# Eight gate projections of the first attention branch computed as four pairs of quarter products, `mid` emitted one step later, and all copies of transposed probabilities on ScalarE

## The chip, the cores and the metric

The kernel runs on one core of one Trainium2 chip. The metric is the device time of the program in microseconds (us); lower is better. A core has five engines that each work through their own queue of instructions in order: TensorE (PE in the profile; its weight loads are listed apart as PEld), VectorE (DVE), ScalarE (ACT), GpSimd (POOL) and SyncE (SP), which here issues most of the DMA transfers. Engines wait for each other through semaphores.

## The reference

One layer of a streaming encoder, for 1024 tokens of a new stream (prompt) and 64 tokens of a running one (sample, with 512 cached tokens), all in float32. The model width is 1024, and each branch has 8 heads of 64.

```python
h = rms_norm(x, norm_w) @ w_in            # 6144 columns:
# sb_q sb_k sb_v sb_z (512 each) | cb_q cb_k cb_v cb_z (512 each) | g_sb g_cb (1024 each)

def stick_breaking(q, k, v):              # first branch, "sb": all earlier keys
    z = q @ k.T * 0.125
    # weight[t,s] = sigmoid(z[t,s]) * product over s<j<t of (1 - sigmoid(z[t,j]))

def band_attention(q, k, v, rel_bias):    # second branch, "cb": nine chunks of 64 keys
    s = q @ k.T * 0.125 + bias            # q and k normed per head
    p = softmax(s)

b_sb = (o_sb * silu(z_sb)) @ w_proj_sb
b_cb = (o_cb * silu(z_cb)) @ w_proj_cb
y = x + (sigmoid(g_sb) * b_sb + sigmoid(g_cb) * b_cb) @ w_out
```

It also returns new keys and values of both branches. The cached keys and the relative bias are scaled up, so that scores are large.

## The kernel before

Every float32 operand of a projection is split into a high part (rounded to the fast matmul format) and a low part (the rest), and a product is made as high x high + high x low + low x high. So a product over 128 rows takes three matmuls. "Prep" of a weight block is a ScalarE copy (high) and a subtraction on GpSimd (low).

The program runs through these stages:

1. **Normed tokens and natural projections** (matmuls at L464): RMSNorm, transposes, and the columns whose result is wanted with tokens on partitions (values of both branches, queries and keys of the second).
2. **Quarter products** (L544 to L658; matmuls at L634): a list `pairs` of column blocks of 256. The block is cut in two halves of columns, the tokens in two halves, the contraction in two halves, and the eight quarter products that this would need are replaced by seven products of sums and differences (a Strassen scheme). Each product has two chunks of tokens (256 and 288 columns), four steps of contraction and three matmuls a step. Before the change `pairs` holds eight entries: keys and queries of the first branch (kinds `"k"`, `"q"`) and the SiLU gates of both branches (`"silu"`). `emit` (L565) evicts a result by its kind, and its code for a kind `"sig"`, a sigmoid without the multiplication, is there already. `prep` and `presum` (L391 to L437) make the operands, `load_raw` (L379) loads the weights, and after the last pair the first gate unit (`load_unit(0)`).
3. **Attention** (L663 to L1205). The tokens are nine tiles: eight of 128 and the sample's 64, called t = 8. The list `seq` (L991) has 144 steps, in the order branch, pair of heads, tile (the sample first), head: 72 of the first branch, then 72 of the second. A step's row length is 128 to 1024 columns in the first branch and 128 to 640 in the second.
4. **Merging and output projection** (L1207 on).

A step of attention is spread over several turns of the loop at L1169:

- `qk(i)` (L1002): scores on TensorE (L1024, L1025). In the first branch ScalarE takes two sigmoids of them (L1027 into `kp`, L1028 into `be`). In the second VectorE adds the bias and finds the row's extreme (L1030), and ScalarE takes the exponential with its sum (L1034).
- `mid(i)` (L1037), on VectorE alone: in the first branch a scan over the row (L1044) and a multiplication (L1045), in the second a reciprocal (L1047) and a scaling (L1048).
- `tr(i)` (L1055), three turns after `qk(i)` (`LAG = 3`): transposes of the probabilities on TensorE into PSUM (L1076) and copies into `wT`. A counter `flip` gives each copy to ScalarE (L1085) or VectorE (L1087): of the first branch's every fourth goes to VectorE, of the second's every other one.
- `av` (L1096): weights times values for two tiles and both heads (L1115), then one multiplication with the SiLU gate on VectorE (L1118).
- `fill(n)` (L978): `n` matmuls from a generator, `run_fill` (L766), which hold TensorE busy between these. The generator first computes gate `units`, one block of 128 columns each, with 72 matmuls (three chunks of tokens with 384, 384 and 320 columns, eight steps of contraction, three matmuls; L773). `ev_act` (L745) evicts a chunk with one ScalarE activation (L748) and stores it. Behind the units it starts the first branch's projection (L873, evicted on VectorE at L877). Before the change there are 16 units, eight of each branch.

One turn `i` emits, in this order: `qk(i)`, loads, half of the turn's filler, `av` if two tiles are complete, `tr(i-3)`, `mid(i)`, the other half of the filler. Each engine executes what it is given in the order of emission. Six calls of `fill(24)` ahead of the loop (two units) cover the first loads.

How much filler a turn gets is written out by hand: `n_sb` matmuls over the first branch and `n_cb` (and 24 more) over the second, shared out by row length (`wt`, `tot`, `amount`, L1161 to L1190). `FP` = 180 is the part of the projection that is reached inside the loop; the rest follows after it (L1278). One more rule: `fill` holds the last unit back, and owes its matmuls, until the flag `late["sb"]` is set at L1191, in the sixth step of the second branch, because the last unit starts loads of the first branch's results (L775).

```python
                        if ci == k == n == 0 and j + 1 == len(units):
                            load_og("sb", 0, late["y"])
...
        while n > 0:
            if prog[0] == len(units) - 2 and "sb" not in late:
                owed[0] = n
                return
```

Scores in PSUM have three buffers (`psZ`), transposes two (`psT`), `be` four, `kp` three and `wT` four.

Of the kernel before, what the change touches and what calls it, by code (L numbers as in the profile page):

```python
# [10 lines left out]
AF = mybir.ActivationFunctionType  # L11
# [6 lines left out]
KT = 8  # L18
# [14 lines left out]
def hybrid_step_kernel(ctx: ExitStack, tc: tile.TileContext, x_prompt, x_sample, c_sbk, c_sbv, c_cbk, c_cbv,  # L33
# [3 lines left out]
    V, A, G, TE, SP = nc.vector, nc.scalar, nc.gpsimd, nc.tensor, nc.sync  # L37
# [15 lines left out]
    def rows(t):  # L53
        return 128 if t < 8 else NS
# [26 lines left out]
    d_g = {b: [dram.tile([128, T], F32, name=f"d_g{b}{u}") for u in range(KT)] for b in ("sb", "cb")}  # L81
# [63 lines left out]
    pairs = []  # L145
    for p in (0, 2):
        pairs += [("k", 512 + 128 * p, p), ("q", 128 * p, p)]
    for p in (0, 2):
        pairs += [("silu", 1536 + 128 * p, d_z["sb"][p:p + 2]), ("silu", 3584 + 128 * p, d_z["cb"][p:p + 2])]
    units = [("ev_act", 4096 + 128 * j, (AF.Sigmoid, d_g["sb"][j])) for j in range(KT)]  # L150
    units += [("ev_act", 5120 + 128 * j, (AF.Copy, d_g["cb"][j])) for j in range(KT)]

    def put_t(dst, src):
        A.activation(dst[0], src, AF.Copy)
# [43 lines left out]
    with ExitStack() as ph:  # L198
# [251 lines left out]
        for i in range(nb):  # L450
            for ti, t in enumerate(TO):
                r = rows(t)
# [6 lines left out]
                for m, (k, n) in enumerate(steps):  # L459
                    if i == 0 and ti == 0 and m == 4:  # L460
                        prep_b(0)
                    w = W.sp[i, k // 4][n // (ns - 1)][:, k % 4]
# [81 lines left out]
    with ExitStack() as ph:  # L544
# [70 lines left out]
        for i in range(len(pairs)):  # L615
            bank, s1, u2, u3 = {}, {}, {}, {}
            for s in range(7):
# [8 lines left out]
                w = blk.pop(n)  # L626
                for c, (a, b) in enumerate(XC):
                    m = b - a
# [22 lines left out]
                if s == 4:  # L651
                    for c, (a, b) in enumerate(XC):
                        m = b - a
# [324 lines left out]
    def fill(n):  # L978
        n += owed[0]
        owed[0] = 0  # L980
        while n > 0:
# [9 lines left out]
    seq = [(b, p, t, hd) for b in ("sb", "cb") for p in range(NPAIR) for t in [8] + list(range(8))  # L991
           for hd in range(2)]

    def band(b, t):
        if t == 8:
            return 0, 576
        if b == "sb":
            return 0, (t + 1) * 128
        k0 = max(0, t - 4)
        return k0, (t + 1 - k0) * 128  # L1000

    def qk(i):  # L1002
        b, p, t, hd = seq[i]
        key = (b, p)
        r = rows(t)
        k0, n = band(b, t)
        hs = [(0, n)] if n <= 512 else [(0, n // 2), (n // 2, n)]
        be = am.tile([128, NP], F32, name="be", bufs=4)
        if t == 8:
            s, ks, q0 = SQ[key, 3], KS[key, 1], 0  # L1010
        else:
            s, ks, q0 = SQ[key, t // 3], KS[key, 0], (t % 3) * 128
        if b == "sb":
            kp = ax.tile([128, NP + 2], F32, name="kp", bufs=3)
            G.memset(kp[:r, n:n + 1], 0.0)
        else:
            kp = am.tile([128, 4], F32, name="sm", bufs=6)
            bt = BI[2 * p + hd]
            off = 0 if t == 8 else 640 - n
        for j, (x, y) in enumerate(hs):  # L1020
            z = psZ.tile([128, 512], F32, name="z")
            o = k0 * 128
            m = y - x
            TE.matmul(z[:r, :m], s[:, 2 * hd, q0:q0 + r], ks[:, hd, o + x:o + y], start=True, stop=False)  # L1024
            TE.matmul(z[:r, :m], s[:, 2 * hd + 1, q0:q0 + r], ks[:, hd, o + x:o + y], start=False, stop=True)  # L1025
            if b == "sb":
                A.activation(kp[:r, x:y], z[:r, :m], AF.Sigmoid, scale=-0.125)  # L1027
                A.activation(be[:r, x:y], z[:r, :m], AF.Sigmoid, scale=0.125)  # L1028
            else:
                V.tensor_tensor_reduce(be[:r, x:y], z[:r, :m], bt[:r, off + x:off + y], 1.0,  # L1030
                                       BIG if j == 0 else kp[:r, j - 1:j], OP.add, OP.min, kp[:r, j:j + 1])
        if b == "cb":
            j = len(hs) - 1
            A.activation(be[:r, :n], be[:r, :n], AF.Exp, bias=kp[:r, j:j + 1], scale=-1.0, accum_out=kp[:r, 2:3])  # L1034
        st[i] = (be, kp)

    def mid(i):  # L1037
        b, p, t, hd = seq[i]
        r = rows(t)
        k0, n = band(b, t)  # L1040
        be, kp = st[i]
        if b == "sb":
            im = imp[0:64, 960 - n:960] if t == 8 else imp[:, NP - n:NP]
            V.tensor_tensor_scan(kp[:r, n - 1::-1], kp[:r, n - 1::-1], im[:, ::-1], 0.0, op0=OP.mult, op1=OP.add)  # L1044
            V.tensor_tensor(out=be[:r, :n], in0=be[:r, :n], in1=kp[:r, 1:n + 1], op=OP.mult)  # L1045
        else:
            V.reciprocal(kp[:r, 3:4], kp[:r, 2:3])  # L1047
            V.tensor_scalar(be[:r, :n], be[:r, :n], kp[:r, 3:4], None, op0=OP.mult)  # L1048

    def wbase(b, j):  # L1050
        return max(0, 2 * j - 4) if b == "cb" and j < 4 else 0

    flip = [0]

    def tr(i):  # L1055
        b, p, t, hd = seq[i]
        r = rows(t)
        k0, n = band(b, t)
        be, _ = st.pop(i)
        j = t // 2 if t < 8 else 4  # L1060
        q0 = (t % 2) * 128 if t < 8 else 0
        s0 = k0 - wbase(b, j)
        nblk = (n + 127) // 128
        groups = {}
        for kb in range(nblk):
            groups.setdefault((s0 + kb) // 4, []).append(kb)
        for g, kbs in groups.items():
            wk = (b, p, j, hd, g)
            if wk not in wT:
                wT[wk] = ak.tile([128, 4, 256], F32, name="wT", bufs=4)  # L1070
            w = wT[wk]
            pt = psT.tile([128, 4, 128], F32, name="pt")
            kr = 128
            for x, kb in enumerate(kbs):
                kr = min(128, n - kb * 128)
                TE.transpose(pt[:kr, x, :r], be[:r, kb * 128:kb * 128 + kr], ident[:r, :r])  # L1076
            m = len(kbs)
            sl = (s0 + kbs[0]) % 4
            if kr < 128:
                m -= 1  # L1080
                A.activation(w[:kr, sl + m, q0:q0 + r], pt[:kr, m, :r], AF.Copy)
            if m:
                flip[0] += 1
                if flip[0] % 2 or b == "sb" and flip[0] % 4:
                    A.activation(w[:, sl:sl + m, q0:q0 + r], pt[:, :m, :r], AF.Copy)  # L1085
                else:
                    V.tensor_copy(w[:, sl:sl + m, q0:q0 + r], pt[:, :m, :r])  # L1087


    def load_z(b, p, j):  # L1090
        zt = am.tile([128, 256], F32, name="zt", bufs=3)
        nq = 256 if j < 4 else 64
        SP.dma_start(zt[:, :nq], d_z[b][p][:, 256 * j:256 * j + nq])
        zts[b, p, j] = zt
# [51 lines left out]
    def load_bias(h):  # L1146
        bt = late["y"].tile([128, 640], F32, name="bias", bufs=4)
        src = d_rb[h][0:1, 127:128]
        SP.dma_start(bt, bass.AP(tensor=src.tensor, offset=src.offset, ap=[[767, 128], [1, 640]]))
        G.memset(bt[0:64, 576:640], BIG)  # L1150
        G.memset(bt[64:128, 0:64], BIG)
        BI[h] = bt
# [5 lines left out]
        flush()  # L1158
        f()
    FP = 180  # L1160
    n_sb = 72 * 7  # L1161
    n_cb = 72 * (len(units) - 9) + FP
    wt = {"sb": lambda n: n, "cb": lambda n: n + 150}
    tot = {b: sum(wt[b](band(b, t)[1]) for bb, p, t, hd in seq if bb == b) for b in ("sb", "cb")}
    amount = {"sb": n_sb, "cb": n_cb}
# [2 lines left out]
    avq = []  # L1168
    for i in range(len(seq) + LAG + 1):  # L1169
        m = 0  # L1170
        if i < len(seq):
            b, p, t, hd = seq[i]
            if b == "cb" and p == 0 and t == 8 and hd == 0:
                sbx.close()
                yst = ExitStack()
                late["y"] = yst.enter_context(tc.tile_pool(name="ay", bufs=2))
                load_bias(0)
                load_bias(1)
            qk(i)
            if hd == 0:  # L1180
                if t % 2 == 1 or t == 8 and (b, p) != ("sb", 0):
                    load_z(b, p, t // 2 if t < 8 else 4)
                prefetch(b, p, t)
            acc += amount[b] * wt[b](band(b, t)[1]) / tot[b]
            if (b, p, t) == ("cb", 0, 8):
                acc += 12
            m = int(acc) - emitted
            emitted += m
        flush()
        if i < len(seq) and seq[i][:3] == ("cb", 0, 1) and hd == 1:  # L1190
            late["sb"] = True  # L1191
        fill(m // 2)
        while avq:
            av(*avq.pop(0))
        if 0 <= i - LAG < len(seq):
            tr(i - LAG)
            b, p, t, hd = seq[i - LAG]
            if hd == 1 and (t % 2 == 1 or t == 8):
                avq.append((b, p, t // 2 if t < 8 else 4))
        if i < len(seq):  # L1200
            mid(i)
        fill(m - m // 2)
    flush(True)
    yst.close()
# [172 lines left out]
    for i in range(2):  # L1377
# [3 lines left out]
        for q, s in enumerate(OP_):  # L1381
# [14 lines left out]
            for c in range(2) if s != "b" else ():  # L1396
# [9 lines left out]
                p = ps[:]  # L1406
# [17 lines left out]
                if s in (3, 4, 5, 6):  # L1424
                    w, half = {3: (0, 0), 4: (1, 1), 5: (1, 0), 6: (0, 1)}[s]
# [3 lines left out]
                    if s == 4:  # L1429
                        p, x = u3[c], xrs.pop((i, 1, 1, c))  # L1430
                    V.tensor_tensor(out=y, in0=p, in1=x, op=OP.add)
                    store_y(i, w, half, c, y)
            for s_, wh, wl in ([] if n == 0 else [(0,) + first, (3, wh, wl)] if n == 1 else
                               [(s, wh, wl)] if s in (0, 3, "b", 5) else []):
                w = 0 if s_ in (0, 3) else 1
                r = 0 if s_ in (0, "b") else 1
# [55 lines left out]
```

## Time and profile before

| | |
|---|---|
| median of 3 runs | 1008.02 us (1007.42 to 1011.17) |
| profiled execution | 1008.24 us, of which the span from first to last instruction is 1006.3 |
| granted TensorE clock, mean | 0.997 |
| busy: PE, DVE, ACT, POOL | 978.0, 655.2, 473.1, 322.0 us |
| HBM traffic | 167 GB/s over the span |

Times in the profile's rows are microseconds unless marked ns, and L773 is line 773 of the kernel. A row of the groups has line, engine, operation, the tiles it writes and reads, a shape and a count, and then after the bars the busy time, the mean ns of one, the idle time of the engine just ahead of them and what ended that idle time. "+5 forms" says that other shapes are in the same row. A row of the table of stages has the stretch, its length, each engine's busy time with its count of instructions, the granted TensorE clock as a share of full speed, the mean busy share of the DMA engines, and GB/s. A row of the timeline has start, duration, engine, line and operation, and in brackets an idle time with what ended it. The chain is the work that ended last, followed back from the end of the program.

### The profile page before, as it was taken

The numbers are of one execution on the slowest core, as the hardware profiler recorded it, in microseconds if no ns is written. First come the engines' busy times: TensorE is split into PE (matmuls) and PEld (weight loads), VectorE is DVE, ScalarE is ACT, GpSimd is POOL, SyncE is SP. The second block draws the span as 40 slices with busy tenths as digits, with TensorE's granted clock in tenths as the row PEclk, the third lists the DMA queues.
The fourth block names the chain that finished last, engine by engine and source line by source line (L and its number), as shares of the span: only waits on it lengthen the run. The fifth ranks groups of instructions, "written<-read, shape, count | busy, mean of one in ns | idle before, by whom it ended". The sixth has DMA issues, their size and how long they took to land.

```text
span 1006.3 us, 20170 instructions
## 1 busy us (share of the span) xinstructions
PE 978.0 (97%) x7512; PEld 929.9 (92%) x7512; DVE 655.2 (65%) x1233; ACT 473.1 (47%) x1075; POOL 322.0 (32%) x338
## 2 busy tenths in 40 slices
PE   5999999999999999999999999999999899989998
PEld 5999999999889999988898878898989798989998
DVE  5466673894354554189798878465766766399735
ACT  5544443444343433277666656454445543366220
POOL 3276663205343543211111101110202200387452
PEclk9999999999999999999999999999999999999999
DMA  6736577434555332697565644775756954863632
GB/s 227 231 105 211 184 247 275 129 100 155 173 163 165 119 98 77 173 244 192 137 169 149 160 116 119 206 201 152 192 151 184 266 168 130 250 213 100 194 128 95
DMA packets 180865, 169.83 MB, mean 169 GB/s; under 512 B 34912, under 2 KB 167136, under 8 KB 180640
## 3 DMA queue, kind: packets, MB, share of 16 engines
q1 hardware_dynamic: 172048, 160.23, 53.7%
q10 hardware_dynamic: 8720, 8.33, 2.6%
q8 instruction: 59, 0.97, 0.4%
q14 instruction: 38, 0.31, 0.1%
HBM read 109.78 MB, written 58.72 MB: 167 GB/s over the span
## 4 chain that ended last, share of the span: by engine, by line
PE 86%; DMA 4%; DVE 3%; ACT 3%; issue 2%; SPq 1%; POOL 1%; DVEq 0%; ACTq 0%
PE acc L464 19%; PE acc L773 17%; PE b L634 15%; PE b L1404 8%; PE o L1115 7%; PE pt L1076 6%; PE b L917 4%; PE z L1025 3%; PE z L1024 3%; PE acc L873 3%; DMA d_ksbT<-hl 1%; PE pk L349 1%; DMA wrawx<-in_w_in_dram 1%; PE pt L277 1%; DVE be L1045 1%
## 5 line engine op out<-in xcount | busy, mean ns | idle before, releaser
L122 POOL TENSOR_TENSOR wlo<-wraw,whi 128x1024 fp32r<-128x1024 f32 x30 | 74.2, 2472 | 245.0 <-ACT whi L115 211.4
L773 PE MATMUL acc<-xm,whi 128*128 128x384 f32 (+1 forms) x384 | 128.6, 335 | 0.0
L1044 DVE TENSOR_TENSOR_SCAN kp<-kp,imp 64x576 f32<-64x576 f32 (+8 forms) x72 | 102.8, 1428 | 21.2 <-ACT kp L1027 21.0
L1034 ACT ACTIVATE be<-be,sm 128x640 f32<-128x640 f32 (+5 forms) x72 | 50.8, 705 | 97.0 <-DVE sm L1030 97.0
L1076 PE MATMUL pt<-ident,be 128*128 128x128 f32 (+2 forms) x608 | 89.5, 271 | 6.2 <-DVE wT L1087 3.4
L1085 ACT ACTIVATE wT<-pt 128x512 f32<-128x512 f32 (+3 forms) x130 | 63.5, 502 | 55.3 <-PE pt L1076 55.3
L1076 PEld LDWEIGHTS pt<-ident,be 128*128 128x128 f32 (+2 forms) x608 | 68.1, 139 | 18.1 <-issue 6.4
L464 PE MATMUL acc<-whi,xa 128*128 128x256 f32 x256 | 74.2, 292 | 0.0
L773 PEld LDWEIGHTS acc<-xm,whi 128*128 128x128 f32 x384 | 72.5, 189 | 1.1
L464 PE MATMUL acc<-wlox,xm 128*128 128x256 f32 x256 | 70.8, 278 | 0.0
L464 PE MATMUL acc<-whi,xm 128*128 128x256 f32 x256 | 70.7, 278 | 0.0
L464 PE MATMUL acc<-wlo,xa 128*128 128x256 f32 x256 | 70.7, 278 | 0.0
L464 PE MATMUL acc<-whix,xb 128*128 128x256 f32 x256 | 70.6, 278 | 0.0
L464 PE MATMUL acc<-whix,xm 128*128 128x256 f32 x256 | 70.6, 278 | 0.0
L1115 PE MATMUL o<-wT,vp 128*64 128x256 f32 (+1 forms) x608 | 67.2, 361 | 0.1
L1045 DVE TENSOR_TENSOR be<-be,kp 64x576 f32<-64x576 f32 (+8 forms) x72 | 60.3, 837 | 10.3 <-DVE kp L1044 0.5
L1027 ACT ACTIVATE kp<-z 128x384 f32<-128x384 f32 (+6 forms) x112 | 54.3, 484 | 24.3 <-PE z L1025 22.9
L773 PE MATMUL acc<-xa,wlo 128*128 128x384 f32 (+1 forms) x192 | 65.4, 341 | 0.0
L773 PE MATMUL acc<-xa,whi 128*128 128x384 f32 (+1 forms) x192 | 65.4, 341 | 0.0
L773 PE MATMUL acc<-xm,wlo 128*128 128x384 f32 (+1 forms) x192 | 65.1, 339 | 0.0
L1115 PEld LDWEIGHTS o<-wT,vp 128*64 128x64 f32 x608 | 43.1, 138 | 23.7 <-issue 8.2
L773 PE MATMUL acc<-xb,whi 128*128 128x384 f32 (+1 forms) x192 | 64.1, 334 | 0.0
(298 smaller groups left out, 3012.6 us busy)
## 6 DMA issues: line engine op xcount, KB each, us to landing
wraw<-in_w_in_dram SPq DMA_DIRECT2D x35, 512.0 KB, 4.5
wrawx<-in_w_in_dram SPq DMA_DIRECT2D x13, 512.0 KB, 4.4
sq<-d_qsbT SPq DMA_DIRECT2D x32, 192.0 KB, 4.8
sq<-d_qcbT SPq DMA_DIRECT2D x32, 192.0 KB, 3.7
gt<-d_gsb SPq DMA_DIRECT2D x30, 192.0 KB, 2.7
xt<-in_x_prompt_dram SPq DMA_DIRECT2D x8, 512.0 KB, 5.7
d_kcbT<-hl SPq DMA_DIRECT2D x8, 512.0 KB, 4.6
d_qcbT<-hl SPq DMA_DIRECT2D x8, 512.0 KB, 5.7
```

Of the source, the lines that this page charges most:

```text
L122: (eng or G).tensor_tensor(out=l, in0=raw, in1=h[:].bitcast(F32), op=OP.subtract)
L464: TE.matmul(ps, x, w, start=m == 0, stop=m == len(steps) - 1)
L634: TE.matmul(ps[:, :m], w[:, hl_, k], right[s](x)[:, k, a:b], start=s < 3 and k == 0 and e == 0, stop=k == 3 and e == 2, skip_group_check=s ...
L773: TE.matmul(ps[:, :b - a], w[:, k], xk(x, k)[:, a:b], start=k == 0 and n == 0, stop=k == KT - 1 and n == 2)
L1027: A.activation(kp[:r, x:y], z[:r, :m], AF.Sigmoid, scale=-0.125)
L1034: A.activation(be[:r, :n], be[:r, :n], AF.Exp, bias=kp[:r, j:j + 1], scale=-1.0, accum_out=kp[:r, 2:3])
L1044: V.tensor_tensor_scan(kp[:r, n - 1::-1], kp[:r, n - 1::-1], im[:, ::-1], 0.0, op0=OP.mult, op1=OP.add)
L1045: V.tensor_tensor(out=be[:r, :n], in0=be[:r, :n], in1=kp[:r, 1:n + 1], op=OP.mult)
L1076: TE.transpose(pt[:kr, x, :r], be[:r, kb * 128:kb * 128 + kr], ident[:r, :r])
L1085: A.activation(w[:, sl:sl + m, q0:q0 + r], pt[:, :m, :r], AF.Copy)
L1115: TE.matmul(o[hd * 64:hd * 64 + 64, c0:c1], vv[:kr, kb, hd * 64:hd * 64 + 64], wT[b, p, j, hd, s // 4][:kr, s % 4, c0:c1], start=si == 0, ...
L1404: TE.matmul(ps[:, t], left[s](xs_, k)[:, ts_], wt_[:, k], start=s < 3 and t == k == e == 0, stop=k == 3 and e == 2, skip_group_check=s > 2 ...
```

## The change

Four edits. The eight sigmoid gates of the first branch leave `units` and join `pairs` as four entries of the kind `"sig"`, so that stage 2 has twelve pairs and `units` eight entries, all of them the second branch's gates. The filler's amounts follow: `n_sb` goes from 504 to 360 matmuls and `n_cb` from 684 to 252. All copies of whole transposed blocks go to ScalarE, and `flip` is gone. `mid` of a step is emitted at the head of the next turn, ahead of that turn's `qk`, and no longer ahead of the last half of its own turn's filler.

```diff
-    units = [("ev_act", 4096 + 128 * j, (AF.Sigmoid, d_g["sb"][j])) for j in range(KT)]
-    units += [("ev_act", 5120 + 128 * j, (AF.Copy, d_g["cb"][j])) for j in range(KT)]
+    pairs += [("sig", 4096 + 128 * p, d_g["sb"][p:p + 2]) for p in range(0, KT, 2)]
+    units = [("ev_act", 5120 + 128 * j, (AF.Copy, d_g["cb"][j])) for j in range(KT)]
...
             if m:
-                flip[0] += 1
-                if flip[0] % 2 or b == "sb" and flip[0] % 4:
-                    A.activation(w[:, sl:sl + m, q0:q0 + r], pt[:, :m, :r], AF.Copy)
-                else:
-                    V.tensor_copy(w[:, sl:sl + m, q0:q0 + r], pt[:, :m, :r])
+                A.activation(w[:, sl:sl + m, q0:q0 + r], pt[:, :m, :r], AF.Copy)
...
-    n_sb = 72 * 7
-    n_cb = 72 * (len(units) - 9) + FP
+    n_sb = 72 * (len(units) - 3)
+    n_cb = 72 + FP
...
     for i in range(len(seq) + LAG + 1):
         m = 0
+        if 0 < i <= len(seq):
+            mid(i - 1)
         if i < len(seq):
             b, p, t, hd = seq[i]
...
-        if i < len(seq):
-            mid(i)
         fill(m - m // 2)
```

More of the change, by code (lines that the diff above doesn't have):

```diff
@@ L1051, in wbase @@
         return max(0, 2 * j - 4) if b == "cb" and j < 4 else 0
-    flip = [0]
     def tr(i):
```

## The prediction

> **What bounds the kernel now.** I read the page first, then the stages, then inside the two attention stages the groups of VectorE and ScalarE, and last the timeline of a few steps.
>
> ```profile
> span 1006.3 us, 20170 instructions
> ...
> PE 86%; DMA 4%; DVE 3%; ACT 3%; issue 2%; SPq 1%; POOL 1%; DVEq 0%; ACTq 0%
> ```
>
> On the page this is a TensorE kernel. The table of stages says how far the other engines are behind. Its rows are: the quarter products; the two gate units ahead of attention; the first branch (its first score matmul stands at 427.17); the second branch (first score matmul at 625.98).
>
> ```profile
> core 0: us, PE busy (x) PEld busy (x) DVE busy (x) ACT busy (x) POOL busy (x), PEclk, DMA share, GB/s
> 226.40:403.60 177.20, 173.25 (x1385) 171.49 (x1385) 87.48 (x174) 68.23 (x159) 81.00 (x56) 1.00 0.45 136
> 403.60:427.17 23.57, 23.57 (x145) 23.56 (x145) 2.16 (x5) 5.27 (x9) 5.72 (x6) 1.00 0.65 172
> 427.17:625.98 198.81, 195.18 (x1403) 172.80 (x1401) 171.78 (x186) 136.21 (x334) 24.36 (x76) 0.99 0.62 164
> 625.98:849.48 223.50, 220.59 (x1602) 200.62 (x1600) 145.79 (x464) 104.30 (x250) 32.54 (x32) 1.00 0.65 184
> ```
>
> TensorE is full in both branches, but only because gate units and projections fill its gaps. In the first branch VectorE is at 171.78 of 198.81, so nearly full too. In the second it is at 145.79 of 223.50, and that looks like room. It isn't, as these two answers show (VectorE, then ScalarE, around the step that starts at 728.87):
>
> ```profile
> 728.87 0.48 DVE L1030 CUSTOM_DVE_ANT_0 be<-z,bias 128x320 f32<-128x320 f32 x1
> 729.28 0.08 DVE L1030 DVE_READ_ACCUMULATOR2_ANT sm<- 128x1 f32 x1
> 729.50 0.55 DVE L1030 CUSTOM_DVE_ANT_0 be<-z,bias,sm 128x320 f32<-128x320 f32 x1
> 729.98 0.08 DVE L1030 DVE_READ_ACCUMULATOR2_ANT sm<- 128x1 f32 x1
> 729.98 0.42 DVE L1087 COPY wT<-pt 128x256 f32<-128x256 f32 x1
> 731.05 0.16 DVE L1047 RECIPROCAL sm<-sm 128x1 f32<-128x1 f32 x1 [0.65 <-ACT be L1034]
> 731.25 0.55 DVE L1048 TENSOR_SCALAR be<-be,sm 128x640 f32<-128x640 f32 x1
> 731.72 0.48 DVE L1030 CUSTOM_DVE_ANT_0 be<-z,bias 128x320 f32<-128x320 f32 x1
> ```
>
> ```profile
> 730.10 0.83 ACT L1034 ACTIVATE be<-be,sm 128x640 f32<-128x640 f32 x1 [1.45 <-DVE sm L1030]
> 730.84 0.18 ACT L1034 ACTIVATION_READ_ACCUMULATOR be<-be,sm 128x1 f32 x1
> ```
>
> This is a ring. VectorE adds the bias and finds the extreme (L1030); ScalarE's exponential (L1034) waits for that; VectorE's reciprocal and scaling (L1047, L1048) wait for the exponential; and the next step's L1030 stands behind them in VectorE's queue. One lap took 731.72 - 728.87 = 2.85 us at 640 columns. It can't be shorter, however idle TensorE is. The groups of the second branch give the ring's whole length, VectorE first, then ScalarE:
>
> ```profile
> L1048 DVE TENSOR_SCALAR be<-be,sm 128x640 f32<-128x640 f32 (+5 forms) x72 | 43.5, 605 | 2.5
> L1030 DVE CUSTOM_DVE_ANT_0 be<-z,bias 128x320 f32<-128x320 f32 (+5 forms) x72 | 34.6, 481 | 9.6 <-PE z L1025 5.9 <-DMA bias<-d_rb 2.8 <-DMA d_gcb<-sg 0.3
> L1030 DVE CUSTOM_DVE_ANT_0 be<-z,bias,sm 128x320 f32<-128x320 f32 (+1 forms) x40 | 21.7, 543 | 5.8
> L1087 DVE COPY wT<-pt 128x256 f32<-128x256 f32 (+3 forms) x51 | 21.0, 412 | 13.7 <-PE pt L1076 13.4
> L1047 DVE RECIPROCAL sm<-sm 128x1 f32<-128x1 f32 (+1 forms) x72 | 11.4, 158 | 17.2 <-ACT be L1034 16.7
> L1030 DVE DVE_READ_ACCUMULATOR2_ANT sm<- 128x1 f32 (+1 forms) x112 | 9.1, 81 | 0.0
> L877 DVE TENSOR_TENSOR xm<-acc,gt 128x384 f32<-128x384 f32 (+1 forms) x17 | 9.0, 531 | 0.0
> L1118 DVE TENSOR_TENSOR zt<-o,zt 128x256 f32<-128x256 f32 (+1 forms) x20 | 7.7, 384 | 23.1 <-PE o L1115 23.1
> ```
>
> ```profile
> L1034 ACT ACTIVATE be<-be,sm 128x640 f32<-128x640 f32 (+5 forms) x72 | 50.8, 705 | 97.0 <-DVE sm L1030 97.0
> L1085 ACT ACTIVATE wT<-pt 128x512 f32<-128x512 f32 (+3 forms) x53 | 25.9, 491 | 16.1 <-PE pt L1076 16.1
> L1034 ACT ACTIVATION_READ_ACCUMULATOR be<-be,sm 128x1 f32 (+1 forms) x72 | 13.4, 187 | 0.0
> ```
>
> 43.5 + 34.6 + 21.7 + 11.4 + 9.1 + 50.8 + 13.4 = 184.5 us of ring in a stage of 223.5. Whatever work is taken off TensorE here, the stage doesn't fall with it below about that.
>
> **The change part by part.** Quarter products. The two kinds of filler, on the chain:
>
> ```profile
> 302.21 101.38 PE b L634 x816
> 403.60 23.73 PE acc L773 x144
> ```
>
> A pair is 7 products of 2 chunks x 12 = 168 matmuls, at 101.38/816 = 0.1242 us, 20.87 us; four make 83.5 us. By the stage's whole time per pair (177.20/8 = 22.15, with its stalls) they would make 88.6. I take 83.5: the stretch quoted, which holds the four SiLU pairs, ran without a gap, and the new pairs are those without the multiplication. What they load, store and issue equals what two units do each (1 MB, twelve stores), so the DMA queue sees the same work earlier. The eight units that go cost 72 x 23.73/144 = 11.87 us each, 94.9 in all. If TensorE stayed the bound everywhere, the kernel would gain 11.4.
>
> But the 83.5 us are certain, since they stand in a stage of their own where TensorE is the bound, while the 94.9 come out of the attention stages. The two units before attention stay. The first branch's filler falls from 504 matmuls to 360 (23.7 us at 0.1648), the second's from 684 + 24 to 252 + 24 (71.2 us).
>
> First branch. Its VectorE groups:
>
> ```profile
> L1044 DVE TENSOR_TENSOR_SCAN kp<-kp,imp 64x576 f32<-64x576 f32 (+8 forms) x72 | 102.8, 1428 | 21.2 <-ACT kp L1027 21.0
> L1045 DVE TENSOR_TENSOR be<-be,kp 64x576 f32<-64x576 f32 (+8 forms) x71 | 59.0, 832 | 10.2 <-DVE kp L1044 0.5 <-PE z L1025 0.5
> L1087 DVE COPY wT<-pt 128x256 f32<-128x256 f32 (+3 forms) x24 | 11.2, 468 | 2.1 <-PE pt L1076 2.0
> L1118 DVE TENSOR_TENSOR zt<-o,zt 128x256 f32<-128x256 f32 (+1 forms) x19 | 7.2, 379 | 11.7 <-PE o L1115 10.1 <-DMA sq<-d_qsbT 1.6
> ```
>
> TensorE alone would let the stage fall to 198.8 - 23.7 = 175.1. VectorE needs 171.8 - 11.2 (the copies that leave) + 10.2 (the gaps ahead of L1045) = 170.8, and 182.5 if it still waits 11.7 for attention outputs. The two are level and the long rows are VectorE's, so I take 179.5: a gain of 19.3, between 16.3 and 23.7.
>
> Second branch. The ring has no step for what leaves. Its lower end is the clean lap. In the quoted lap the scaling took 0.55, while its mean at this shape is 749 ns:
>
> ```profile
> L1048 DVE TENSOR_SCALAR be<-be,sm 128x640 f32<-128x640 f32 x32 | 24.0, 749 | 1.1
> ```
>
> The lap's rows with that mean add to 0.48 + 0.08 + 0.55 + 0.08 + 0.83 + 0.18 + 0.16 + 0.75 = 3.11; it took 2.85, or 0.916 of it: 184.5 x 0.916 = 169. Between 169 and 184.5 I take 177. On top stay the wait for the first bias (2.8); a third of the 23.1 for attention outputs (7.7), for TensorE now runs ahead; and a new one. After the first branch exactly one unit is left, and the filler holds that back until the first branch's results are stored, five steps into the second. Some 37 matmuls fall due at once, 6.1 us in one step, where a lap is 184.5/72 = 2.6 on average: 3.5 us. Together 191, a gain of 32.5. Bounds: 169 + 5 = 174 (gain 49.5), and 184.5 with all of its waits, 23.1 + 5.9 + 2.8, is 216.3 (gain 7.2).
>
> The step's move. `mid` issues VectorE instructions alone, no DMA. It goes from ahead of a step's last filler to ahead of the next step's scores, so on VectorE's queue it passes only that filler's work (L877, the low parts of the first branch's outputs). It still stands ahead of the next L1030, so the ring stays closed. L877's 9.0 us now lie between L1030 and the reciprocal, under the exponential (0.83 + 0.18); without that cover they would return as up to 9.0. On TensorE the transposes, three steps behind, still find `mid` in the step after its own.
>
> The copies. VectorE loses 21.0 us and a wait of 13.4 in the second branch, 11.2 and 2.0 in the first. ScalarE takes them at about its own price for such copies (491 ns against 412), some 25 and 12 us. Queued behind them are evictions and the next exponential; VectorE waits for the latter. ScalarE stood idle 1.45 us ahead of the exponential quoted, so I cost it at nothing; without that cover it would be up to 25 in the ring.
>
> Sum: 83.5 - 19.3 - 32.5 = +31.7. The profiled execution took 1008.24 us (span 1006.3), the median run 1008.02, 0.2 less: **1039.7**. The ends together: 83.5 - 23.7 - 49.5 = +10.3 (1018.3), and 88.6 - 16.3 - 7.2 = +65.1 (1073).
>
> One thing speaks for worse. In the first branch a gap of TensorE was followed by a halved clock:
>
> ```profile
> 580.27 1.15 PE L1076 MATMUL pt<-ident,be 128*128 128x128 f32 x8 [2.40 <-DVE wT L1087]
> ```
>
> ```profile
> 581.20:584.60 3.40, 3.40 (x16) 2.13 (x16) 1.66 (x4) 1.30 (x4) 0.20 (x2) 0.50 0.00 0
> ```
>
> [...]
>
> **The rivals.** (1) TensorE stays the bound throughout: 1008.0 - 11.4 = **996.6**. For it speaks the 86% of the chain; against it the ring, which needs 169 us at the least where TensorE's work would be 220.6 - 71.2 = 149.4. It decides if the second branch ends up near 152 (223.5 - 71.2).
> (2) The ring opens, because the later `mid` does let the next L1030 pass while the exponential runs. Then the branch follows TensorE's 149.4 with some 8 of waits, 157.5 and a gain of 66: 83.5 - 19.3 - 66 = -1.8, **1006**, no change that can be told. Against it is the order of emission in the diff.
> (3) The gaps that the ring leaves (149.4 of 191 busy) halve the clock again and again. With half the time at half clock TensorE's 149.4 become 149.4/0.75 = 199, and with the 14 us of waits above the branch takes 213, a gain of 10.5: +53.7, **1061.7**. Against it: a busier TensorE is what follows a halving, and 3.4 us later the clock was back.
>
> **How the numbers follow.** The forecast has 0.83, rival (1) 0.05, (2) 0.04, (3) 0.08. The range 1017 to 1060 takes in the lower end and most of the upper one; the two fast rivals and most of (3) lie outside. About 0.5% (5 us) is what a measurement here can tell from no change. Faster: rival (1) and a little of (2), 0.06. Same: the rest of (2), 0.03. Slower: 0.91.
>
> **What would show it.** The quarter products should run 83 to 89 us longer with no new gap. In the second branch laps at 640 columns should stay at 2.85 to 2.95, start to start of L1030, with TensorE's busy share near 0.8 and the branch at 185 to 200 us; the exponential's wait for L1030 should stay its main wait. The first branch should last 175 to 183. I am wrong if steps fall towards 157.5/72 = 2.2 on average (rivals 1 and 2), or if the branch is long with the granted clock under 0.95 (rival 3).

## The result, and the profile after

The changed kernel is slower: 1048.15 us median (1045.6 to 1050.31, 4 runs) against 1009.39 for the kernel before in the same comparison, a ratio of 1.0384 with a 95% interval of 1.035 to 1.0417. The profiled execution took 1045.6 us, 37.4 more than that of before. The page's span and chain:

```profile
span 1043.7 us, 20626 instructions
...
PE 77%; DVE 7%; ACT 6%; DMA 4%; issue 4%; SPq 2%; POOL 0%; DVEq 0%; ACTq 0%
```

TensorE's share of the chain fell from 86% to 77%; VectorE's rose from 3% to 7% and ScalarE's from 3% to 6%. The table of stages (columns as before: length, busy time of each engine, granted clock, DMA share, GB/s); the rows are the quarter products, the two units, the two branches and all that follows:

```profile
226.40:488.30 261.90, 258.05 (x2056) 256.30 (x2055) 117.34 (x232) 99.54 (x228) 119.01 (x84) 0.99 0.42 126
488.30:511.87 23.57, 23.57 (x145) 23.56 (x145) 1.37 (x2) 4.74 (x8) 5.72 (x6) 1.00 0.70 190
511.87:684.14 172.27, 170.00 (x1260) 148.40 (x1257) 157.78 (x160) 137.09 (x350) 20.50 (x74) 1.00 0.65 173
684.14:886.28 202.14, 166.22 (x1165) 134.03 (x1162) 123.28 (x414) 105.56 (x277) 18.49 (x26) 0.97 0.62 170
886.28:1043.70 157.42, 150.42 (x1148) 148.02 (x1148) 98.01 (x132) 60.16 (x98) 77.61 (x47) 1.00 0.51 160
```

The quarter products cost 261.90 - 177.20 = 84.7 us. The first branch gave back 198.81 - 172.27 = 26.5, the second only 223.50 - 202.14 = 21.4, where 71.2 us of TensorE's work had left it. The rest grew by 0.6 (156.8 before). 84.7 - 26.5 - 21.4 + 0.6 = 37.4. In the second branch TensorE is busy for 166 of 202 us, VectorE for 123 and ScalarE for 106: nobody is full. One lap of the ring, VectorE's timeline in the third quarter of that branch:

```profile
785.28 0.48 DVE L1030 CUSTOM_DVE_ANT_0 be<-z,bias 128x320 f32<-128x320 f32 x1
785.69 0.08 DVE L1030 DVE_READ_ACCUMULATOR2_ANT sm<- 128x1 f32 x1
785.92 0.55 DVE L1030 CUSTOM_DVE_ANT_0 be<-z,bias,sm 128x320 f32<-128x320 f32 x1
786.40 0.08 DVE L1030 DVE_READ_ACCUMULATOR2_ANT sm<- 128x1 f32 x1
787.47 0.16 DVE L1047 RECIPROCAL sm<-sm 128x1 f32<-128x1 f32 x1 [0.99 <-ACT be L1034]
787.67 0.55 DVE L1048 TENSOR_SCALAR be<-be,sm 128x640 f32<-128x640 f32 x1
788.14 0.48 DVE L1030 CUSTOM_DVE_ANT_0 be<-z,bias 128x320 f32<-128x320 f32 x1
```

788.14 - 785.28 = 2.86 us, as before the change. The copy that stood between L1030 and L1047 is gone (0.42 us), and the wait for the exponential has grown by most of it, from 0.65 to 0.99. That is how work that lies under another engine's work looks when it is removed. The groups of VectorE in the second branch say it for all 72 laps (idle time ahead and its cause stand behind the last bar):

```profile
L1048 DVE TENSOR_SCALAR be<-be,sm 128x640 f32<-128x640 f32 (+5 forms) x72 | 37.8, 526 | 2.5
L1030 DVE CUSTOM_DVE_ANT_0 be<-z,bias 128x320 f32<-128x320 f32 (+5 forms) x72 | 34.5, 480 | 5.6 <-DMA bias<-d_rb 2.9 <-PE z L1025 2.2 <-DMA zt<-d_zcb 0.2
L1030 DVE CUSTOM_DVE_ANT_0 be<-z,bias,sm 128x320 f32<-128x320 f32 (+1 forms) x40 | 21.7, 543 | 5.8
L1047 DVE RECIPROCAL sm<-sm 128x1 f32<-128x1 f32 (+1 forms) x72 | 11.6, 161 | 41.6 <-ACT be L1034 41.5
```

L1030 waits for scores for 2.2 us in all, so TensorE is not late; L1047 waits 41.5 for the exponential, where it had waited 16.7.

### The profile page after: what moved, and what is told of

The parts are those of the page before. It is cut to its first block, busy times and chain, and to the rows that moved or that the text cites. A ratio compares the mean times of both kernels' runs of the same rounds, so it can differ in the third digit from the quotient of the medians.

```text
span 1043.7 us, 20626 instructions
## 1 busy us (share of the span) xinstructions
PE 984.6 (94%) x7608; PEld 925.1 (89%) x7608; DVE 644.5 (62%) x1211; ACT 507.5 (49%) x1189; POOL 342.6 (33%) x358
## 4 chain that ended last, share of the span: by engine, by line
PE 77%; DVE 7%; ACT 6%; DMA 4%; issue 4%; SPq 2%; POOL 0%; DVEq 0%; ACTq 0%
PE b L634 22%; PE acc L464 18%; PE acc L773 8%; PE b L1398 7%; PE o L1109 6%; PE pt L1074 5%; PE b L917 3%; ACT be L1034 3%; DVE be L1030 3%; PE z L1024 2%; PE z L1025 2%; ACT wT L1081 1%; DVE kp L1044 1%; DVE be L1048 1%; DMA d_ksbT<-hl 1%
## 5 line engine op out<-in xcount | busy, mean ns | idle before, releaser
L122 POOL TENSOR_TENSOR wlo<-wraw,whi 128x1024 fp32r<-128x1024 f32 x22 | 55.1, 2503 | 210.8 <-ACT whi L115 163.4
L1044 DVE TENSOR_TENSOR_SCAN kp<-kp,imp 64x576 f32<-64x576 f32 (+8 forms) x72 | 97.1, 1349 | 22.0 <-ACT kp L1027 22.0
L1081 ACT ACTIVATE wT<-pt 128x512 f32<-128x512 f32 (+3 forms) x208 | 88.9, 464 | 42.3 <-PE pt L1074 41.9
L1034 ACT ACTIVATE be<-be,sm 128x640 f32<-128x640 f32 (+5 forms) x72 | 50.7, 705 | 79.6 <-DVE sm L1030 79.0
L1109 PE MATMUL o<-wT,vp 128*64 128x256 f32 (+1 forms) x608 | 75.4, 359 | 11.8 <-ACT wT L1081 11.8
L1109 PEld LDWEIGHTS o<-wT,vp 128*64 128x64 f32 x608 | 44.6, 137 | 41.0 <-ACT wT L1081 20.9
L1045 DVE TENSOR_TENSOR be<-be,kp 64x576 f32<-64x576 f32 (+8 forms) x72 | 64.1, 890 | 10.3 <-ACT kp L1027 0.5
L1024 PE MATMUL z<-ks,sq 128*128 128x320 f32 (+4 forms) x192 | 63.5, 333 | 6.6 <-DVE sm L1030 6.6
L773 PE MATMUL acc<-xm,whi 128*128 128x384 f32 (+1 forms) x192 | 65.1, 339 | 0.0
L1025 PE MATMUL z<-ks,sq 128*128 128x320 f32 (+4 forms) x192 | 62.6, 329 | 0.0
L642 DVE TENSOR_TENSOR u<-b,s 128x256 f32<-128x256 f32 (+1 forms) x48 | 21.0, 441 | 63.9 <-PE b L634 63.5
L1028 ACT ACTIVATE be<-z 128x384 f32<-128x384 f32 (+6 forms) x112 | 56.5, 504 | 0.0
L464 PEld LDWEIGHTS acc<-whi,xa 128*128 128x128 f32 x256 | 47.9, 188 | 0.1
```

The lines of the kernel that those rows point to most:

```text
L464: TE.matmul(ps, x, w, start=m == 0, stop=m == len(steps) - 1)
L773: TE.matmul(ps[:, :b - a], w[:, k], xk(x, k)[:, a:b], start=k == 0 and n == 0, stop=k == KT - 1 and n == 2)
L1109: TE.matmul(o[hd * 64:hd * 64 + 64, c0:c1], vv[:kr, kb, hd * 64:hd * 64 + 64], wT[b, p, j, hd, s // 4][:kr, s % 4, c0:c1], start=si == 0, ...
```

## The experiments

Each kernel was run beside the kernel before on the same chip. The lengths of branches are read from one profile each; where a kernel had one run, its time has no interval.

**ring_open: does the order on VectorE's queue set the second branch?** All of the change stays, but `mid` of the step before is emitted behind this step's scores and bias pass, not ahead of them.

```diff
-        if 0 < i <= len(seq):
+        last = i == len(seq) or i < len(seq) and seq[i] == ("cb", 0, 8, 0)
+        if i and last:
             mid(i - 1)
...
             qk(i)
+            if i and not last:
+                mid(i - 1)
```

> The changed kernel with mid of the step before emitted behind this step's scores instead of ahead of them, so that VectorE's bias pass of a step no longer stands behind the wait for the exponential of the step before (at the boundary of the branches it stays ahead). Ring theory (VectorE and ScalarE in turn set the second branch): the second branch falls from 202 us to what TensorE needs, 150 and some waits, 160 to 172; laps at 640 columns fall from 2.85 to 2.1 to 2.4; the whole kernel takes 1004 to 1018 us instead of 1048. Rival, ScalarE (the copies that moved there hold up the transposes): the branch stays within 5 us of 202, for ScalarE does the same work. Rival, TensorE's clock (the halving at the boundary and the gaps): the branch falls by 10 us at the most, the part that the halved clock took.

Measured: 1019.59 us median, 1.0099 of before (1.0067 to 1.0131). The second branch took 175.1 us instead of 202.1. Both are a little over what was expected (1004 to 1018, 160 to 172). Its row, and the row of its part from the second pair of heads on:

```profile
684.44:859.51 175.07, 159.50 (x1165) 135.18 (x1162) 122.16 (x414) 105.46 (x277) 18.48 (x26) 0.97 0.72 197
...
746.00:859.51 113.51, 107.99 (x804) 91.29 (x800) 83.42 (x292) 68.41 (x182) 8.63 (x11) 1.00 0.75 199
```

Every engine carries out as many instructions as in the changed kernel (1165, 414 and 277 on TensorE, VectorE and ScalarE), and 27 us are gone. From 746 on TensorE is busy for 108 of 113.5 us, so it is the bound again. VectorE's wait ahead of the reciprocal fell from 41.6 us to 0.2, and its wait for scores rose from 2.2 to 16.2. The median lap at 640 columns fell from 2.90 us to 2.24; a short one takes 1.78 (VectorE's groups, then its timeline; L1047 stands right behind L1030 and belongs to the step before):

```profile
L1030 DVE CUSTOM_DVE_ANT_0 be<-z,bias 128x320 f32<-128x320 f32 (+5 forms) x72 | 34.7, 482 | 19.5 <-PE z L1025 16.2 <-DMA bias<-d_rb 2.9
...
L1047 DVE RECIPROCAL sm<-sm 128x1 f32<-128x1 f32 (+1 forms) x72 | 11.3, 157 | 0.2 <-ACT be L1034 0.2
```

```profile
802.95 0.48 DVE L1030 CUSTOM_DVE_ANT_0 be<-z,bias 128x320 f32<-128x320 f32 x1
803.36 0.08 DVE L1030 DVE_READ_ACCUMULATOR2_ANT sm<- 128x1 f32 x1
803.59 0.55 DVE L1030 CUSTOM_DVE_ANT_0 be<-z,bias,sm 128x320 f32<-128x320 f32 x1
804.07 0.08 DVE L1030 DVE_READ_ACCUMULATOR2_ANT sm<- 128x1 f32 x1
804.07 0.16 DVE L1047 RECIPROCAL sm<-sm 128x1 f32<-128x1 f32 x1
804.26 0.55 DVE L1048 TENSOR_SCALAR be<-be,sm 128x640 f32<-128x640 f32 x1
804.73 0.48 DVE L1030 CUSTOM_DVE_ANT_0 be<-z,bias 128x320 f32<-128x320 f32 x1
```

So the order set the branch. The rival of ScalarE's copies falls, since ScalarE still makes them all, and so does that of the clock: the branch's mean granted clock is 0.97 in both kernels.

**recip2: is idle VectorE time in that branch free?** The changed kernel with the reciprocal doubled (`V.reciprocal(kp[:r, 3:4], kp[:r, 2:3])` on two lines).

> The changed kernel with the reciprocal in mid (second branch, 72 steps) emitted twice, the second one giving the same values: 0.16 us of VectorE work a step, 11.6 in all, where VectorE is busy 123 of 202 us. Ring theory: it lies in every lap, so the second branch gets 11 to 14 us longer (214 to 216) and the kernel 1057 to 1062; laps at 640 columns go from 2.85 to 3.0. Rivals (ScalarE or TensorE sets the branch): VectorE has 79 us of idle time there, so under 4 us.

Measured: 1062.49 us (one run), second branch 217.6, both just above the expected ranges. Its row and the two reciprocals:

```profile
685.55:903.16 217.61, 174.13 (x1165) 137.97 (x1162) 134.95 (x486) 105.73 (x278) 18.44 (x26) 0.94 0.57 158
```

```profile
L1048 DVE RECIPROCAL sm<-sm 128x1 f32<-128x1 f32 (+1 forms) x72 | 11.8, 163 | 2.5
L1047 DVE RECIPROCAL sm<-sm 128x1 f32<-128x1 f32 (+1 forms) x72 | 11.6, 161 | 40.9 <-ACT be L1034 40.6
```

11.8 us of added work, with 2.5 of gaps ahead of it, made the branch 15.5 us longer although VectorE is idle for some 80 us of it. The shortest lap at 640 columns went from 2.85 to 3.04 us, and 72 laps with 0.19 more are 13.7 of the 15.5. Idle time inside a ring isn't spare.

**fp60: is TensorE's time in that branch free?** The changed kernel with `FP = 60` in place of 180.

> The changed kernel with FP at 60 instead of 180: 120 matmuls of the projection, 19.8 us of TensorE, leave the second branch and follow behind it. Ring theory: the branch keeps its length within 5 us of 202, the stretch behind it grows by 19 us, and the kernel takes 1060 to 1068. Rival, TensorE sets the branch (by its clock or its work): the branch falls by 15 to 20 and the kernel stays within 5 us of 1046 to 1050.

Measured: 1072.51 us (one run). The second branch and what follows it:

```profile
687.20:888.51 201.31, 153.29 (x1045) 118.40 (x1042) 116.64 (x404) 103.91 (x275) 13.28 (x24) 0.93 0.55 150
888.51:1070.70 182.19, 172.38 (x1268) 169.37 (x1268) 104.09 (x141) 61.80 (x100) 81.81 (x49) 0.99 0.52 162
```

120 matmuls fewer shortened the branch by 0.8 us; the same matmuls behind it cost 24.8 where 19 were expected, so the kernel's time lies above its range too. The granted clock in the branch fell from 0.97 to 0.93 and the branch did not get longer, which speaks against the clock as its bound. This is the change itself once more: work moved from where it was hidden to where it isn't.

**gates_only and mid_back: the parts of the change.** gates_only has the gate pairs and the amounts of filler alone; mid_back has these and the copies, with `mid` where it stood before.

> The kernel before with the four gate pairs and the new amounts of filler alone; the copies alternate and mid stands as before. Ring theory: VectorE's 54 copies lie in the ring where they outlast the exponential or wait for the transposes, so the second branch takes 205 to 220 instead of 202, the first 175 to 183 instead of 172, and the kernel 1050 to 1070. Rival, ScalarE: without the copies there the branch gets shorter than 202 and the kernel takes 1030 to 1043.

> The changed kernel with mid where it stood before, ahead of the last half of its own step's filler; gates and copies as changed. Ring theory: the order of bias pass and mid on VectorE is the same, only the projection's 16 products (L877, 8.6 us) come out of the exponential's cover and into the lap: second branch 202 to 211, kernel 1045 to 1058. Rival, the later mid is itself what costs (the transposes wait for it): the branch falls below 195 and the kernel below 1041.

Measured: 1060.51 and 1051.69 us (one run each). The branches of gates_only, then those of mid_back:

```profile
511.73:695.02 183.29, 172.42 (x1259) 148.70 (x1257) 167.64 (x186) 131.14 (x326) 21.41 (x74) 1.00 0.61 162
695.02:900.63 205.61, 170.80 (x1170) 135.13 (x1167) 138.47 (x463) 91.90 (x227) 18.50 (x26) 0.97 0.60 168
```

```profile
514.47:686.75 172.28, 170.00 (x1259) 148.40 (x1257) 157.78 (x160) 137.10 (x350) 20.57 (x74) 1.00 0.65 173
686.75:893.09 206.34, 169.87 (x1165) 136.76 (x1162) 123.02 (x414) 105.57 (x277) 18.74 (x26) 0.95 0.59 167
```

With the gates alone the branches took 183.3 and 205.6; the copies brought the first to 172.3 and left the second at 206.3; the later `mid` brought that to 202.1. So the copies help by 11 us and the later `mid` by about 4, and the gates cost it all. The 4 us fit the 16 products of L877 (8.5 us), which the later `mid` puts under the exponential and so out of the lap: laps with an L877 and nothing else added run 3.7 us over clean laps in mid_back and 0.6 in the changed kernel. But 4 us is little to tell apart by one profile each.

**ring_open_before and copies_only: what is an open ring worth while TensorE is full?** The first is the kernel before with all copies on ScalarE and the edit of ring_open; the second has the copies alone.

> The kernel before, its sixteen gate units and its amounts of filler kept, with all copies on ScalarE and mid of the step before emitted behind this step's scores. Ring theory: with full filler TensorE sets both branches (195 of 199 and 221 of 224 us busy), so an open ring has only TensorE's few idle us to give: 1001 to 1008 us, 0 to 8 us less than before; the second branch 216 to 222. Rival, the ring's opening is worth its 27 us everywhere: 980 to 985.

> The kernel before with all copies on ScalarE and nothing else. ring_open_before gained in the first branch alone (198.8 to 193.2 us; the second 223.5 and 223.7), where the open ring changes nothing on VectorE's queue. So the copies alone should give the same: first branch 192 to 195, second 222 to 226, 1001 to 1006 us. Rival: that gain needed the later mid as well, and the kernel stays at 1007 to 1011.

Measured: 1003.03 us, a ratio of 0.9942 (0.9921 to 0.9964), and 1002.26, 0.9925 (0.9898 to 0.9953). The second branch of ring_open_before, then both of copies_only:

```profile
620.04:843.77 223.73, 220.03 (x1604) 200.34 (x1602) 127.89 (x413) 118.22 (x303) 32.99 (x32) 1.00 0.65 185
```

```profile
428.60:621.83 193.23, 192.49 (x1404) 171.25 (x1402) 162.66 (x162) 143.00 (x358) 22.76 (x76) 1.00 0.64 168
621.83:843.06 221.23, 219.43 (x1597) 199.62 (x1595) 125.13 (x412) 117.18 (x300) 33.48 (x32) 1.00 0.66 185
```

The second branch took 223.7 and 221.2 against 223.5, each just outside what was expected of it: the ring, opened or closed, is worth nothing under TensorE's full load. The first fell by 5.6 us in both, to 193.2. The copies alone make a kernel that takes 0.75% less than the one before, and so less than the changed one; from ring_open_before it can't be told apart.

**two_pairs: half of the trade, on the open ring.** Four gates as two pairs, four as units; `n_sb = 72 * 5`, `n_cb = 72 * 5 + FP`.

> The kernel ring_open with half of the trade: four of the eight sigmoid gates as two pairs of quarter products, four as units ahead of the other branch's eight; filler for five units in the first branch (as after the change) and for five units and the projection's 180 in the second. Ring theory: two pairs cost 42.4 us, the first branch stays at 172 (26.5 less than before), the second loses 144 matmuls (23.7 us) and is set by TensorE at 194 to 200, with filler at its start and no burst: 996 to 1006 us. Rival (the quarter products can't pay, whatever the ring does): 1010 or more.

Measured: 1003.94 us, 0.9949 (0.9931 to 0.9967). The quarter products and the second branch:

```profile
226.40:446.36 219.96, 216.26 (x1721) 214.44 (x1720) 102.06 (x204) 84.29 (x194) 101.94 (x70) 0.99 0.43 130
...
642.36:844.98 202.62, 197.45 (x1453) 177.51 (x1450) 124.12 (x414) 113.30 (x293) 27.85 (x30) 0.99 0.68 191
```

The second branch, with TensorE busy for 197.5 of 202.6 us, is a little longer than expected. It gave 20.9 us back for 23.7 taken, where ring_open gave back 48.4 for 71.2. But what the trade itself is worth shows beside ring_open_before, which has the same order and copies without it: the two pairs cost 42.8 us, the first branch gave back 21.0 (172.3 against 193.2), the second 21.1, and 1003.94 us can't be told from 1003.03. So half of the trade, on the open ring, neither pays nor costs; the gain against the kernel before is that of the copies. That the quarter products can pay isn't shown.

**spare_unit and half_unit: what keeps ring_open above the kernel before?** Both move filler from the first branch to the second, 72 and 36 matmuls.

> The kernel ring_open with one unit more for the second branch: n_sb 288 instead of 360, n_cb 324 instead of 252. TensorE then has filler in the first five steps of the second branch, where it had none and its clock was halved for 10 us. If the loss of ring_open against before (some 10 us) is the empty start and the burst behind it: the first branch 161 to 168, the second 178 to 182, in all 1010 to 1017. Rival: the first branch is already VectorE's (158 of 172 busy) and hardly falls, the second grows by 12: 1022 to 1030.

> The kernel ring_open with half a unit (36 matmuls, 5.9 us) moved from the first branch to the second, which are about the matmuls that fall due in the second branch's first five steps: no burst, and the first branch keeps most of its filler. spare_unit moved 72 and gained 3 us in the first branch, where VectorE stopped it, and gave back 2 in the second. If the empty start and the burst cost ring_open 5 us or more: first branch 169 to 171, second 168 to 173, 1010 to 1016 us. Rival: as for spare_unit, what one branch gains the other gives back: 1017 to 1021.

Measured: 1019.07 us for spare_unit, 1.0098 of before as ring_open's 1.0099 (its branches 169.0 and 176.9), so my expectation missed, and the rival's range too; and 1013.16 for half_unit, 1.0027 (1.0015 to 1.004), as expected. The branches of half_unit:

```profile
511.55:681.33 169.78, 164.31 (x1223) 143.23 (x1221) 156.24 (x160) 136.12 (x349) 21.34 (x73) 1.00 0.66 174
681.33:853.14 171.81, 162.21 (x1200) 139.46 (x1198) 123.55 (x414) 105.67 (x278) 18.72 (x28) 0.98 0.73 201
```

The first branch gives back 2.5 us for 36 matmuls and 3.2 for 72; VectorE is busy for 156 and 154 us of it, and that this is its limit isn't shown. In the second, 36 matmuls more made the branch 3.3 us shorter. What went is the end of the burst: VectorE's wait ahead of L839 fell from 5.6 us in ring_open to 1.5. The start did not get cheaper (VectorE's first bias pass stands 8.8 us behind the first scores, 7.3 in ring_open). So the amounts in this change leave a little filler in the wrong branch.

## Why the prediction was right, point by point

**Quarter products:** +83.5 forecast, +84.7 measured. The eight older pairs lost 1.7 us to the clock by my estimate, half of a stretch of 3.41 us at half speed (0.50), behind a stall that was there before (1.80 us, now 2.28); the new pairs ran without a gap (on the chain 1488 matmuls in 186.39 us from 301.91 on).

**First branch:** a gain of 19.3 forecast, within 16.3 and 23.7; 26.5 measured, over the upper end. Three things were off. VectorE's wait for attention outputs, of which I kept 11.7 us in the worse case, fell to 2.1. TensorE's own limit, 175.1, was too high: it kept 3.6 us of idle time and a stretch of 3.40 us at half clock, and after the change TensorE is idle for 2.3 us and its clock is 1.00. And the stage ends with TensorE's first scores of the second branch, which VectorE reaches later than before: the first L1030 stands 7.2 us behind them (5.0 before), and that time is booked to the second branch.

**Second branch:** a gain of 32.5 forecast, 21.4 measured. The mechanism held: laps at 640 columns took 2.85 us at the least and 2.90 in the median, and recip2 and ring_open show that the laps set the branch. The sum behind the gain had two errors that partly cancel.

The ring was put at 177, between 169 by the clean lap and 184.5 by the sum of its rows. In the profile after, the rows add to 178.8 us (37.8 + 34.5 + 21.7 + 11.6 + 50.7 of the exponential + 13.4 and 9.1 of the two readouts). But rows that follow one another overlap a little (785.28 + 0.48 against 785.69 in the lap above), and a few scalings took up to 1.88 us. The shortest lap of each width, taken for all steps of that width (576, 128, 256, 384, 512, then 640 columns), gives 8 x (2.67 + 1.25 + 1.56 + 1.86 + 2.17) + 32 x 2.85 = 167.3 us. So the clean lap was the better measure, the sum of the rows is no floor, and 177 was some 10 us too much.

What lies on top of the laps was too small: 14 us forecast, 202.1 - 167.3 = 34.8 measured. Three rows carry most of it, the start of VectorE, the end of the burst and the multiplication of the attention outputs (two lines of VectorE's timeline, one of its groups):

```profile
691.37 0.45 DVE L1030 CUSTOM_DVE_ANT_0 be<-z,bias 64x288 f32<-64x288 f32 x1 [2.86 <-DMA bias<-d_rb]
...
710.85 2.08 DVE L839 TENSOR_TENSOR xb<-ot,xa 128x384 fp32r<-128x384 f32 x1 [5.75 <-ACT xa L834]
```

```profile
L1112 DVE TENSOR_TENSOR zt<-o,zt 128x256 f32<-128x256 f32 (+1 forms) x21 | 8.1, 384 | 15.3 <-PE o L1109 15.3
```

The start costs 691.37 - 684.14 = 7.2 us where I had put the 2.8 for the bias; VectorE is still in the last long rows of the first branch. The burst costs more than its matmuls: it finishes a chunk of the last unit, the low part of the first branch's outputs (L839) falls due with it, and VectorE stands 5.75 us ahead of that with the next `mid` behind. That lap is 7.7 us longer than a clean one; I had put 3.5. And the other laps with an L1112 are 14.8 us longer than clean ones; VectorE waits 15.3 us for attention outputs where I had kept a third of 23.1, because TensorE would run ahead. It does not run ahead there: it waits 11.2 us for ScalarE's copies (L1081) before its products for these outputs (L1109). The remaining 5 us are spread over many laps.

**The sum:** +31.7 us forecast, +37.4 measured between the two profiles (38.8 between the medians). That it came so near is in part luck. The first branch gained 7.2 us more than forecast and the second 11.1 less; and inside the second, 10 us too much for the ring stood against 21 too little on top of it. Both branches lie just outside the lengths that I had named as signs, 172.3 against 175 to 183 and 202.1 against 185 to 200.

**Copies and `mid`:** costed at nothing in the second branch. gates_only and mid_back bear that out for the copies, with 205.6 and 206.3 us. I compared ScalarE's and VectorE's price for them by group means of mixed shapes (491 ns against 412); by shape ScalarE was no slower, with 395 ns against 422 at 128x256 and 602 against 684 at 128x512, and between those two kernels its busy time in the branch rose by 13.7 us and not by 25. In the first branch the copies are worth 11 us between gates_only and mid_back. The 11.2 us that leave VectorE stood in my sum; what had no term is that VectorE's queue held up TensorE, which waited 9.0 us for L1087's copies in gates_only and 3.0 in the kernel before.

**Rivals.** That TensorE stays the bound (996.6) fell with the row of the second branch. That the later `mid` opens the ring (1006) fell with the laps of 2.86 us; ring_open shows that an order which does open it existed, two lines further down; even then the kernel takes 1019.59 us, since the start and the burst stay and the second branch takes 175 us where this rival had 157.5. The halving clock (1061.7) had a part, for which my sum has no term; that half of TensorE's time would pass at half speed was an assumption, and no run shows it. The mean clock of the second branch fell to 0.97, and the boundary has 10.24 us at half speed. But TensorE waits there anyway (it is busy for 4.98 of them), ring_open gained 27 us with the same mean clock, and fp60 had a lower one (0.93) in a branch of the same length.

## What to carry to other kernels

Before work is taken off the engine that looks full, add up the longest ring of waits in that stage: operations of two in-order engines that wait for each other and that the next step queues behind. Measure it by the shortest laps and not by the sum of their rows. It stays a floor for as long as the order does (with a closed ring the shortest lap at 640 columns took 2.85 us before and after the change), and no share of busy time shows it; here it was 167 us of a stage of 202 in which the three engines were busy for 166, 123 and 106. Then look for what else stands in the laps: here waits for attention outputs, a late start and one burst made up most of the other 35. Whether a step is emitted "one later" matters only by what it passes on its own queue: past the filler it was worth about 4 us (single runs), past the next step's first operation 27. And where TensorE was full, the same opening was worth nothing.

## What the runs showed of the hardware

The granted clock of TensorE was 0.50 behind some of its gaps and stayed at 1.00 behind others of about the same length. The same wait ahead of the transposes at L595, twice in the kernel before, with the stretch that followed the second:

```profile
254.46 0.85 PE L595 MATMUL acc<-ident,u 128*128 128x128 f32 x4 [2.15 <-ACT ko L601]
...
301.25 0.44 PE L595 MATMUL acc<-ident,u 128*128 128x128 f32 x2 [1.80 <-ACT ko L601]
```

```profile
302.90:306.30 3.40, 3.40 (x30) 3.40 (x29) 1.41 (x3) 0.99 (x4) 2.42 (x2) 1.00 0.81 214
```

And in the kernel after:

```profile
300.95 0.44 PE L595 MATMUL acc<-ident,u 128*128 128x128 f32 x2 [2.28 <-ACT ko L601]
```

```profile
302.60:306.01 3.41, 3.41 (x18) 3.41 (x16) 0.42 (x1) 0.99 (x4) 2.39 (x2) 0.50 0.73 215
```

Gaps of 1.80 and 2.15 us left the clock alone (it was 1.00 from 254.4 to 262 us too), one of 2.28 was followed by 3.41 us at half speed (0.50). In the gap of 6.04 us at the branches' boundary (685.84 to 691.88) the clock fell 2.5 us after its start and stayed down for 10.24 us:

```profile
688.31:698.55 10.24, 4.98 (x22) 4.34 (x22) 4.06 (x17) 4.64 (x11) 0.58 (x4) 0.50 0.83 237
```

The length of a single gap doesn't decide it here. From 767 to 770 us of the changed kernel the clock was 0.50 as well, and the longest gap in the 12 us ahead of that was of 1.46 us, behind two matmuls and one of 0.37:

```profile
766.64 1.41 PE L1109 MATMUL o<-wT,vp 128*64 128x256 f32 x6 [1.46 <-ACT wT L1081]
```

What does decide it, no run here shows.
